# Four memory-attention heads turned so that queries lie on the partitions, in a one-core hybrid decoder step

## The chip, the cores and the metric

The kernel runs on one core of a Trainium2 chip. The metric is the device time of one execution in microseconds (us). The engines are called as in the profile: PE (TensorE matmuls), PEld (its weight loads), DVE (VectorE), ACT (ScalarE), POOL (GpSimd) and SP (SyncE, which issues most of the transfers).

## The reference, cut to what matters

One layer: a combined input projection, a gated convolution, eight dilated window-attention heads, four memory heads, a gate, one output projection, a residual and a final norm. The change touches the memory heads and the output projection's weights:

```python
def _mem_attn(qm, mk, mv):                       # 4 heads of 64, 2048 queries, 256 memory tokens
    s = jnp.einsum('bthe,bmhe->bhtm', qm, mk) * (HEAD_DIM ** -0.5)
    p = jax.nn.softmax(s, axis=-1)
    return jnp.einsum('bhtm,bmhe->bthe', p, mv)

def _finish(x, conv_y, attn_o, mem_o, z, w_out):
    mix = jnp.concatenate([conv_y, attn_o, mem_o], axis=-1) * jax.nn.silu(z)
    return x + mix @ w_out
```

## The kernel before, in words

After the projections come twelve "units": `Head` 0 to 7 (window attention) and `MemHead` 0 to 3. A unit has two parts, `scores()` and `values()`; while one unit's scores run, the values of the unit before it run too (`period`). A value is split into a high and a low half wherever a product has to be exact, so scores are two accumulating matmuls (`qk`), and an output product is three.

A memory head before the change keeps the 256 memory tokens on the partitions (two blocks of 128) and the queries along the row. Its maximum per query therefore runs across partitions. `Maxima.add` takes a transposing reduction on DVE (L765), `Maxima.finish` reduces again (L770), turns on PE (L772), reduces (L774), writes 4 KB to DRAM (`dmax`, L775) and reads it back to all partitions as `Rm` (L776). POOL then subtracts `Rm` (L1078), ACT takes the exponential (L1079), PE multiplies by the memory values (L1083), and `Sums` adds the weights over the partitions with matmuls against ones (L789). `finish_head` turns these sums, takes reciprocals, spreads and turns them again (L802 to L818), scales the output and stores it to `dmix` (L821).

The window heads use the same path for their maximum. Their POOL subtractions are L955, L956, L961, L976 and L977, their value products L950, their exponentials L957, L958, L962, L978, L982. `values()` of a head is cut by `yield` into places: the subtractions for the first half of `Rm` stand at place 0, `mx.finish(1)` and all other subtractions at 0.1, the products from 0.60 on.

Order: inside `tc.manual_schedule` (the periods of heads 1 to 7) PE and SP run in the order of the program text. On the other engines, and everywhere outside it, a planner fixes a static order per engine: among the instructions that are ready in its own model of time, the one that comes first in the text goes first. [...]

The tiles of even units come from `vals[0]` and `keys[0]`, those of odd ones from `vals[1]` and `keys[1]`. After the last unit the output stage starts: `load_wo` brings `w_out` in 16 pieces of 256 KB (L1188), splits each on ACT (L1189) and on DVE or POOL (L1190). `Rows` loads a block of mixed rows (`mx`, L1223), gates and splits it (L1224 to L1228), and runs 48 products a block over eight chunks (L1236, L1246); 17 blocks make 816 products. Row blocks 16, 0 and 1 start beside the last memory head:

```python
    interleave(units[-2].values(), lw, 6, 16)
    p2v.close()
    ow = ctx.enter_context(tc.tile_pool(name="ow", bufs=2, side="right", reuse_waits="tile"))
    ...
    interleave(units[-1].values(), first_rows(), 6, 80)
```

Of the kernel before, what the change touches and what calls it, by code (L numbers as in the profile page):

```python
# [18 lines left out]
D = 1024  # L19
T = 2048  # L20
# [6 lines left out]
EPS = 1e-6  # L27
SLOPE = [2.0 ** -(h + 1) for h in range(H)]
# [246 lines left out]
def tile_step(ctx, tc, x_prompt, x_sample, mem_prompt, ck, cv, cconv, cmk, cmv, g_in, w_in, conv_w,  # L275
# [448 lines left out]
    p2q = ctx.enter_context(ExitStack())  # L724
    vals[0] = p2v.enter_context(tc.tile_pool(name="vals0", bufs=1, side="right", reuse_waits="tile"))
# [15 lines left out]
    def q_load(row, turn):  # L741
        qh = keys[turn].tile([128, T], R, name="qh")
        ql = keys[turn].tile([128, T], R, name="ql")
# [286 lines left out]

    class MemHead:
        def __init__(self, h, turn):
            self.h, self.turn = h, turn

        def load_qk(self):
            h = self.h
            self.q = q_load(512 + h * 64, self.turn)
            self.mk = mk = keys[self.turn].tile([128, T], R, name="ks").rearrange("p (a b) -> p a b", b=128)[:, 0:2]
# [3 lines left out]
        def load_v(self):  # L1042
            pass
# [4 lines left out]
        def scores(self):  # L1048
            vp, mk, (qh, ql) = vals[self.turn], self.mk, self.q
            Rm = vp.tile([128, T], F, name="Rm")  # L1050
            mx = Maxima(self.turn, Rm, 2)
            S = {}
            for hf in range(2):
                for kb in range(2):
                    S[kb, hf] = vp.tile([128, 8, 128], F, name="S", bufs=4)
                for q in range(2):
                    for kb in range(2):
                        ps = psQ.tile([128, 4, 128], F, name="qk")
                        c = 1024 * hf + 512 * q
                        qk(ps, mk[:, kb], qh[:, c:c + 512], ql[:, c:c + 512])  # L1060
                        nc.scalar.activation(S[kb, hf][:, 4 * q:4 * q + 4], ps, AF.Copy)  # L1061
                    yield
                for kb in range(2):
                    mx.add(mx.parts[:, 32 * hf:32 * hf + 32, kb], S[kb, hf].rearrange("p r (x c) -> p (r x) c", c=32))
            self.S, self.Rm = S, Rm.rearrange("p (r b) -> p r b", b=128)
            for hf in range(2):
                mx.finish(hf)
                yield

        def values(self):  # L1070
            h, S, Rm = self.h, self.S, self.Rm
            po = psA.tile([128, 2, 512], F, name="acc")
            sums = Sums()
            o_sb = wk.tile([128, 8, 128], F, name="osb", bufs=1)
            o_v = o_sb.rearrange("p (a r) (J b) -> p r a J b", r=2, b=8)
            for hf in range(2):
                for kb in range(2):
                    nc.gpsimd.tensor_sub(S[kb, hf], S[kb, hf], Rm[:, 8 * hf:8 * hf + 8])  # L1078
                    nc.scalar.activation(S[kb, hf], S[kb, hf], AF.Exp)  # L1079
                yield 0.25 + 0.4 * hf  # L1080
                for kb in range(2):
                    for g in range(2):
                        nc.tensor.matmul(po[g * 64:(g + 1) * 64, hf], memv[:, kb, h * 64:(h + 1) * 64],  # L1083
                                         S[kb, hf][:, 4 * g:4 * g + 4].rearrange("p x y -> p (x y)"),
                                         start=(kb == 0), stop=(kb == 1), skip_group_check=True)
                nc.scalar.activation(o_v[:, hf], po[:, hf].rearrange("p (J a b) -> p a J b", a=4, b=8), AF.Copy)
            for kb in range(2):
                for r4 in range(4):
                    sums.add(r4, 0, 512, S[kb, r4 // 2][:, 4 * (r4 % 2):4 * (r4 % 2) + 4].rearrange("p x y -> p (x y)"), last=kb == 1)
            yield from finish_head(o_sb, sums, 768 + h * 64, 1.2)  # L1090
# [44 lines left out]
    units = [Head(h, h % 2) for h in range(H)] + [MemHead(h, h % 2) for h in range(HM)]  # L1135
# [6 lines left out]
    keys[1].pool = p2q.enter_context(tc.tile_pool(name="keys1", bufs=1, reuse_waits="tile"))  # L1142
    units[1].regroup(16, range(4))

    def loads(n):
# [3 lines left out]
        for k in range(2):  # L1149
# [3 lines left out]
            if k == 0:  # L1153
                units[n].load_v()
        for k in range(2):
# [10 lines left out]
    periods(H, len(units) - 1, 6)  # L1166
    advance(9.0)
    with tc.high_priority(350):
        for _ in units[-1].scores():
            pass  # L1170
# [4 lines left out]
    CH = range(8)  # L1175
    woh, wol = {}, {}

    room = [hT["A"][0].rearrange("p s c n -> p (s c n)")[:, D * i:D * i + D] for i in range(6)]
    for d in reversed(CH):
# [153 lines left out]
```

## Time and profile before

| what | us |
|---|---|
| median of 3 runs (lowest, highest) | 1350.94 (1350.39, 1357.62) |
| the profiled execution, its own time | 1356.83 |
| span of the profiled execution | 1354.8 |
| PE busy over the span | 1235.3 (91%) |
| stretch of the memory heads (1047 to 1172): PE busy of 125 us | 102.38 |

The profile counts an engine as busy while an instruction of its runs; a busy PE is not a PE at its peak, because matmuls overlap. "Idle before" is the time that an engine stood still in front of an instruction, with what released it. The granted clock (PEclk) is a share of 2.4 GHz, 0.50 being 1.2 GHz. Times within the trace count from the start of the span.

### The profile page before, as it was taken

The page shows a single profiled execution, that of the slowest core. Times are in us where ns is not written, and L with a number is a line of the kernel's source. Part 1 is how long each engine was busy: PE and PEld are TensorE (multiplying, and loading weights), DVE is VectorE, ACT ScalarE, POOL GpSimd, SP SyncE. Part 2 cuts the span into 40 slices and gives each one's busy share as a digit, 9 for nine tenths or more (in the row PEclk, how much of TensorE's full clock was granted, in tenths as well). Part 3 has the DMA queues.
Part 4 walks back from the last instruction along what each step waited for, and adds up shares of the span by engine and source line. Part 5 has one row for each costly group of instructions (what it writes and reads, how often), then busy time and mean ns, then how long its engine had stood idle before and what let it go on. Part 6 is the DMA issues. An engine that isn't in the chain of part 4 may idle for free. (4 is left out here: it accounts for less than half of the span.)

```text
span 1354.8 us, 20180 instructions
## 1 busy us (share of the span) xinstructions
PE 1235.3 (91%) x7814; PEld 991.2 (73%) x7814; DVE 643.6 (48%) x1201; ACT 435.8 (32%) x692; POOL 460.1 (34%) x398
## 2 busy tenths in 40 slices
PE   6999999999797779999999999898899877999997
PEld 5778898988696666777898787666666432778886
DVE  4544221156556750400451077777787235554442
ACT  4433132322232001011112217566665555421111
POOL 2130010155455510100470006666666656110000
PEclk9999999999898889999999999899999987999999
DMA  6453142378887437476555477888888856776641
GB/s 232 129 152 105 51 135 100 125 228 247 245 249 248 149 87 167 137 176 194 152 168 158 106 170 172 189 186 188 187 187 179 193 136 180 228 237 191 197 153 66
DMA packets 228103, 229.57 MB, mean 169 GB/s; under 512 B 67348, under 2 KB 182280, under 8 KB 223912
## 3 DMA queue, kind: packets, MB, share of 16 engines
q1 hardware_dynamic: 222248, 217.79, 58.9%
q10 hardware_dynamic: 5760, 10.49, 2.2%
q8 instruction: 62, 1.02, 0.3%
q14 instruction: 33, 0.27, 0.1%
HBM read 171.92 MB, written 56.31 MB: 168 GB/s over the span
## 5 line engine op out<-in xcount | busy, mean ns | idle before, releaser
L359 PE MATMUL b<-hA,whi 128*128 128x384 f32 (+1 forms) x1152 | 288.1, 328 | 7.7 <-DVE big L644 6.1
L359 PEld LDWEIGHTS b<-hA,whi 128*128 128x128 f32 x1152 | 204.7, 190 | 17.7 <-issue 7.0
L359 PE MATMUL b<-hA,wlo 128*128 128x384 f32 (+1 forms) x576 | 188.3, 327 | 0.0
L351 POOL TENSOR_TENSOR wlo<-wraw,whi 128x512 fp32r<-128x512 f32 x56 | 80.8, 1459 | 283.8 <-ACT whi L350 253.1
L359 PE MATMUL b<-hB_hi,whi 128*128 128x512 f32 (+1 forms) x416 | 165.2, 397 | 12.8 <-DVE big L688 8.4
L124 POOL TENSOR_TENSOR spr<-sk,sqb 128x512 f32<-128x512 f32 (+2 forms) x110 | 122.7, 1126 | 145.6 <-DMA sqb<-dqs 56.6
L359 PE MATMUL b<-hB_hi,wlo 128*128 128x512 f32 (+1 forms) x416 | 163.6, 393 | 0.0
L359 PE MATMUL b<-hB_lo,whi 128*128 128x512 f32 (+1 forms) x416 | 163.5, 393 | 0.0
L125 DVE TENSOR_REDUCE sc<-spr 128x8 f32<-128x512 f32 (+1 forms) x160 | 87.7, 571 | 66.5 <-POOL spr L124 66.2
L359 PEld LDWEIGHTS b<-hA,wlo 128*128 128x128 f32 x576 | 109.9, 191 | 4.4 <-issue 3.7
L828 DVE SCALAR_TENSOR_TENSOR S<-dt,b 128x128 f32<-128x128 f32 (+2 forms) x224 | 70.1, 355 | 90.1 <-PE b L825 51.1
L417 POOL TENSOR_TENSOR ss<-ss,nhalf 128x1 f32<-128x1 f32 (+1 forms) x34 | 20.8, 613 | 249.6 <-DVE ss L416 240.6
L359 PEld LDWEIGHTS b<-hB_hi,whi 128*128 128x128 f32 x416 | 80.0, 192 | 31.6 <-DVE big L688 9.2
L359 PEld LDWEIGHTS b<-hB_lo,whi 128*128 128x128 f32 x416 | 79.8, 192 | 19.3 <-issue 2.5
L359 PEld LDWEIGHTS b<-hB_hi,wlo 128*128 128x128 f32 x416 | 80.0, 192 | 17.7 <-issue 2.1
L961 POOL TENSOR_TENSOR S<-S,Rm 128x512 f32<-128x512 f32 x32 | 40.6, 1294 | 141.2 <-DVE S L828 61.4
L765 DVE TRANSPOSE_TENSOR_REDUCE mparts<-S 128x12 f32<-128x384 f32 (+1 forms) x96 | 76.3, 823 | 25.1 <-ACT S L1061 25.0
L695 ACT ACTIVATE ehi<-b 128x384 f32<-128x384 f32 (+2 forms) x40 | 20.7, 518 | 155.9 <-PE b L359 139.1
L1236 PE MATMUL b<-hA,mh 128*128 128x512 f32 x192 | 64.5, 392 | 3.7 <-DVE xo L1266 3.1
L557 DVE TENSOR_TENSOR elo<-big,ehi 128x512 fp32r<-128x512 f32 x24 | 22.4, 969 | 94.5 <-ACT ehi L556 78.6
L350 ACT ACTIVATE whi<-wraw 128x512 fp32r<-128x512 f32 x56 | 33.5, 625 | 92.9 <-PE b L359 87.9
L1236 PE MATMUL b<-woh,ml 128*128 128x512 f32 x160 | 62.8, 394 | 0.0
(250 smaller groups left out, 2412.9 us busy)
## 6 DMA issues: line engine op xcount, KB each, us to landing
sk<-in_cache_win_k_dram SPq DMA_DIRECT2D x72, 256.0 KB, 3.9
vq<-in_cache_win_v_dram SPq DMA_DIRECT2D x36, 512.0 KB, 5.7
wraw<-in_w_in_dram SPq DMA_DIRECT2D x48, 256.0 KB, 4.3
sqb<-dqs SPq DMA_DIRECT2D x48, 256.0 KB, 4.4
Rm<-dmax SPq DMA_DIRECT2D x24, 512.0 KB, 4.6
v<-out_dram SPq DMA_DIRECT2D x16, 512.0 KB, 5.4
zg<-dz SPq DMA_DIRECT2D x16, 512.0 KB, 4.0
xo<-in_x_prompt_dram SPq DMA_DIRECT2D x16, 512.0 KB, 4.5
```

Source lines behind the costliest of these rows:

```text
L124: E.tensor_mul(pr[:n, :width], kt, qt)
L125: nc.vector.tensor_reduce(dst, pr[:n, :width].rearrange("p (h e) -> p h e", e=64), axis=AX.X, op=OP.add)
L350: nc.scalar.activation(hi[:, a:a + 4], raw, AF.Copy)
L351: lo_eng.tensor_sub(lo[:, a:a + 4], raw, f32(hi[:, a:a + 4]))
L359: nc.tensor.matmul(ps, a(d), b(d), start=(n == 0), stop=(n == 23))
L417: nc.gpsimd.tensor_tensor(ss[:n], ss[:n], nhalf[:n], op=OP.pow)
L557: nc.vector.tensor_sub(lo, part, f32(hi))
L695: nc.scalar.activation(zt[:, :n], ps, AF.Silu)
L765: nc.vector.tensor_reduce(out, scores, axis=AX.X, op=OP.max, apply_transpose=True)
L828: nc.vector.scalar_tensor_tensor(S, dt, sl, ps, op0=OP.mult, op1=OP.add)
L961: nc.gpsimd.tensor_sub(S3[:, r4], S3[:, r4], mr[:, r4])
L1236: nc.tensor.matmul(self.ps[k], l[:, d], r[d][:, sl], start=first and i == 0, stop=last and i == 2)
```

## The change

A memory head now keeps 128 queries on the partitions and the 256 tokens along the row. It runs in four groups G of 512 queries. `weights(G)` does the scores with the queries as the stationary operand, takes the maximum along the row from PSUM on DVE, negates it, and lets ACT take the exponential with that bias and its sum (`accum_out`). The weights are scaled by the reciprocal sum, on POOL for even G (one product over 128x1024) and on DVE for odd G (four). `turn(G)` transposes the weights on PE, eight blocks a group, with one copy out of PSUM on ACT and one on DVE. `values(hf)` multiplies by the memory values for two groups and stores the result without any further scaling.

The four heads are one written-out loop of 19 steps inside the manual order of PE and SP, in which step n does `weights` of group n, `turn` of group n-2 and, at even n, `values` of the groups before that. The values of window heads 6 and 7 that are left are spread over these steps (`advance(0.09 * n)`). All four memory heads take their tiles from `vals[0]` and `keys[0]`. Output chunks 0 to 2 are loaded in steps 5 to 10; the other five are loaded after the loop, through two buffers instead of four, and the first row blocks come after all memory heads in the text.

```diff
+EARLY = (0, 1, 2)
...
+    psM, psMQ = Ring((4, 5)), Ring((2, 3))
+
     class MemHead:
...
         def load_qk(self):
-            h = self.h
-            self.q = q_load(512 + h * 64, self.turn)
...
+            h, k = self.h, self.h % 2
+            self.q = q_load(512 + h * 64, 0, *(("ks", "kr") if k else ("qh", "ql")))
...
-        def scores(self):
...
-        def values(self):
...
+        def weights(self, G):
...
+            P = self.P[G] = vals[0].tile([128, 4, 8, 32], F, name="S", bufs=4).rearrange("p t a b -> p t (a b)")
+            m, l = wk.tile([128, 4], F, name="mm"), wk.tile([128, 4], F, name="ml")
+            for i in range(2):
+                ps = psMQ.tile([128, 2, 256], F, name="qk")
+                for k in range(2):
+                    c = 512 * G + 256 * i + 128 * k
+                    nc.tensor.matmul(ps[:, k], qh[:, c:c + 128], mk, start=True, stop=False)
+                    nc.tensor.matmul(ps[:, k], ql[:, c:c + 128], mk, start=False, stop=True)
+                nc.vector.tensor_reduce(m[:, 2 * i:2 * i + 2], ps, axis=AX.X, op=OP.max)
+                nc.vector.tensor_scalar(m[:, 2 * i:2 * i + 2], m[:, 2 * i:2 * i + 2], -1.0, None, op0=OP.mult)
+                for k in range(2):
+                    t = 2 * i + k
+                    nc.scalar.activation(P[:, t], ps[:, k], AF.Exp, bias=m[:, t:t + 1], accum_out=l[:, t:t + 1])
+            nc.vector.reciprocal(l, l)
+            if G % 2:
+                for t in range(4):
+                    nc.vector.tensor_scalar(P[:, t], P[:, t], l[:, t:t + 1], None, op0=OP.mult)
+            else:
+                nc.gpsimd.tensor_mul(P, P, l.unsqueeze(2).to_broadcast([128, 4, 256]))
+
+        def turn(self, G):
...
             for kb in range(2):
...
+                pt = psM.tile([128, 4, 128], F, name="pt")
+                for t in range(4):
+                    nc.tensor.transpose(pt[:, t], self.P[G][:, t, 128 * kb:128 * kb + 128], ident)
+                out = self.PT[G // 2][:, 2 * (G % 2) + kb].rearrange("p (a b) -> p a b", b=128)
+                if kb:
+                    nc.vector.tensor_copy(out, pt)
+                else:
+                    nc.scalar.activation(out, pt, AF.Copy)
+
+        def values(self, hf):
...
+            po = psM.tile([128, 512], F, name="pt")
+            for kb in range(2):
+                for g in range(2):
+                    nc.tensor.matmul(po[g * 64:(g + 1) * 64], memv[:, kb, h * 64:(h + 1) * 64], self.PT[hf][:, 2 * g + kb],
+                                     start=(kb == 0), stop=(kb == 1), skip_group_check=True)
...
+        if n == H - 1:
+            yield 0.6
+            units[H + 1].load_qk()
+            return
...
-    periods(H, len(units) - 1, 6)
...
+        def load_wo(pool, chunks):
...
+                    raw = pool.tile([128, 512], F, name="woraw", bufs=2)
...
+        wo1 = ctx.enter_context(tc.tile_pool(name="wo1", bufs=1, reuse_waits="tile"))
+        lw = load_wo(wo1, EARLY)
+        streams.append([0.0, units[H - 1].values(), 0.0])
+        mem = units[H:]
+        for n in range(4 * HM + 3):
+            advance(0.09 * n)
+            if n < 4 * HM:
+                mem[n // 4].weights(n % 4)
+            if n in (4, 8):
+                mem[n // 4 + 1].load_qk()
+            if n >= 5:
+                next(lw, None)
+            if 2 <= n < 4 * HM + 2:
+                mem[(n - 2) // 4].turn((n - 2) % 4)
+            if n >= 4 and n % 2 == 0:
+                mem[(n - 4) // 4].values((n - 4) // 2 % 2)
+        advance(9.0)
...
+    with tc.high_priority(100):
+        for _ in lw:
             pass
...
+        for _ in load_wo(wo, [d for d in CH if d not in EARLY]):
+            pass
     p2v.close()
...
-    interleave(units[-1].values(), first_rows(), 6, 80)
+    for _ in first_rows():
+        pass
```

## Rows read from the trace of the kernel before

**Rows 1.** Chain that ended last, in order of time: start, us, what

```profile
1215.50 121.10 PE b L1236 x528
1336.61 11.00 PE b L1246 x48
```

**Rows 2.** Busy time by stretch: PE, PEld, DVE, ACT, POOL, then clock, DMA, GB/s

```profile
1047.00:1172.00 125.00, 102.38 (x653) 52.77 (x652) 53.72 (x76) 69.98 (x105) 67.84 (x40) 0.90 0.69 184
1098.00:1104.00 6.00, 1.14 (x4) 0.59 (x4) 1.25 (x1) 0.26 (x1) 1.83 (x1) 1.00 0.87 258
1104.00:1110.00 6.00, 3.86 (x12) 2.30 (x14) 1.51 (x3) 4.75 (x7) 6.00 (x4) 0.50 0.02 5
...
1172.00:1348.00 176.00, 172.48 (x752) 140.62 (x750) 79.19 (x99) 34.22 (x51) 10.84 (x16) 1.00 0.56 174
```

**Rows 3.** Timeline of SP: heads 6 and 7 store their maxima

```profile
1013.92 0.34 SPq L775 DMA_DIRECT2D dmax<-mc  x1
...
1047.67 0.53 SPq L775 DMA_DIRECT2D dmax<-mc  x1
```

**Rows 4.** Timeline of POOL: heads 6 and 7, then memory heads 0 and 3

```profile
1019.49 2.53 POOL L961 TENSOR_TENSOR S<-S,Rm 128x512 f32<-128x512 f32 x2 [10.07 <-DMA Rm<-dmax]
...
1060.81 2.48 POOL L961 TENSOR_TENSOR S<-S,Rm 128x512 f32<-128x512 f32 x2 [17.82 <-DMA Rm<-dmax]
...
1084.06 9.40 POOL L1078 TENSOR_TENSOR S<-S,Rm 128x1024 f32<-128x1024 f32 x4
...
1145.92 5.31 POOL L1078 TENSOR_TENSOR S<-S,Rm 128x1024 f32<-128x1024 f32 x2
```

**Rows 5.** Timeline of DVE and ACT: head 7's `Rm` late; later, row block 16

```profile
1060.65 0.21 DVE L810 RECIPROCAL rl<-b 128x16 f32<-128x16 f32 x1
...
1063.33 1.06 ACT L962 ACTIVATE S<-S 128x1024 f32<-128x1024 f32 x1 [4.66 <-POOL S L961]
1064.29 1.04 ACT L811 ACTIVATE rx<-rl 128x1024 f32<-128x1024 f32 x1
...
1147.03 1.97 DVE L1224 TENSOR_TENSOR mx<-mx,zg 128x256 f32<-128x256 f32 x1
```

**Rows 6.** Timeline of PE: 256-column pairs, four transposes, eight value products

```profile
1020.00 0.29 PE L824 MATMUL b<-hA,kr 128*128 128x256 f32 x1
1020.12 0.29 PE L825 MATMUL b<-hA,kr 128*128 128x256 f32 x1
...
1020.98 0.60 PE L807 MATMUL b<-ident,rx 128*128 128x128 f32 x4
1021.34 0.36 PE L824 MATMUL b<-hA,kr 128*128 128x256 f32 x1
...
1090.56 1.94 PE L1083 MATMUL acc<-S,memv 128*64 128x512 f32 x8
```

**Rows 7.** Busy time of PE, 1047 to 1098: first L950 alone, then L789

```profile
1047.00:1098.00 51.00, 15.67 (x256) 11.40 (x256) 0.97 0.79 182
...
1047.00:1098.00 51.00, 12.58 (x72) 2.12 (x72) 0.97 0.79 182
```

**Rows 8.** ACT and DVE: busy us and mean ns, or ns min/median/max

```profile
L1061 ACT ACTIVATE S<-b 128x512 f32<-128x512 f32 x32 | 18.0, 599 | 13.5 <-PE b L825 8.4 <-PE b L789 4.6 <-PE acc L1083 0.2
L958 ACT ACTIVATE S<-S 128x128 f32<-128x128 f32 x4 | 1.2, 306 | 1.0 <-POOL S L955 1.0
...
L1251 ACT ACTIVATION_READ_ACCUMULATOR sq<-xo x2: 185/186/186, 1343.5 to 1349.0; 128x1 f32 x2
...
L125 DVE TENSOR_REDUCE sc<-spr x160: 401/670/689, 275.4 to 711.2; 128x8 f32<-128x512 f32 x96, 128x4 f32<-128x256 f32 x64
```

**Rows 9.** Landing of `mx` after its issue (L1223), then gating and split

```profile
DMA to landing us min/median/max: 1.8/4.7/7.7
...
L1224 DVE TENSOR_TENSOR mx<-mx,zg 128x896 f32<-128x896 f32 x2 | 2.2, 1094 | 2.4 <-DMA mx<-dmix 2.4
L1227 ACT ACTIVATE mh<-mx 128x1024 fp32r<-128x1024 f32 x1 | 1.1, 1057 | 3.7 <-DVE mx L1224 3.7
```

More of the change, by code (lines that the diff above doesn't have):

```diff
@@ L739, in tile_step, with q_load @@
     d1 = dt1.rearrange("p (r J c) -> p r J c", r=4, J=2)
-    def q_load(row, turn):
-        qh = keys[turn].tile([128, T], R, name="qh")
-        ql = keys[turn].tile([128, T], R, name="ql")
+    def q_load(row, turn, hi="qh", lo="ql"):
+        qh = keys[turn].tile([128, T], R, name=hi)
+        ql = keys[turn].tile([128, T], R, name=lo)
         for g in range(2):
@@ L1039, in load_qk @@
             nc.sync.dma_start(f32(mk[0:64]).rearrange("p a b -> p (a b)"), dmk_hi[h * 64:(h + 1) * 64])
             nc.sync.dma_start(f32(mk[64:128]).rearrange("p a b -> p (a b)"), dmk_lo[h * 64:(h + 1) * 64])
-        def load_v(self):
-            pass
+            self.P, self.PT = {}, {}
         def regroup(self, d, parts):
             pass
-        def scores(self):
[L1049 to L1068, printed above, removed]
@@ L1070, in values @@
-        def values(self):
[L1071 to L1086, printed above, removed]
-            for kb in range(2):
-                for r4 in range(4):
-                    sums.add(r4, 0, 512, S[kb, r4 // 2][:, 4 * (r4 % 2):4 * (r4 % 2) + 4].rearrange("p x y -> p (x y)"), last=kb == 1)
-            yield from finish_head(o_sb, sums, 768 + h * 64, 1.2)
@@ L1133, in period @@
             x[2] += 1.0
-    units = [Head(h, h % 2) for h in range(H)] + [MemHead(h, h % 2) for h in range(HM)]
+    units = [Head(h, h % 2) for h in range(H)] + [MemHead(h) for h in range(HM)]
     units[0].load_qk()
@@ L1165, in tile_step @@
         periods(1, H, 24)
-    periods(H, len(units) - 1, 6)
[L1167 to L1170, printed above, removed]
+        p2k.close()
+        CH = range(8)
+        woh, wol = {}, {}
+        room = [hT["A"][0].rearrange("p s c n -> p (s c n)")[:, D * i:D * i + D] for i in range(6)]
+        def load_wo(pool, chunks):
+            for d in chunks:
+                for x in (woh, wol):
+                    x[d] = room.pop() if room else pool.tile([128, D], R, name="wo%d" % (2 * d + (x is wol)))
+            for d in chunks:
+                for k in range(2):
+                    raw = pool.tile([128, 512], F, name="woraw", bufs=2)
+                    sl = slice(k * 512, (k + 1) * 512)
+                    nc.sync.dma_start(raw, w_out[0][d * 128:(d + 1) * 128, sl])
+                    nc.scalar.activation(woh[d][:, sl], raw, AF.Copy)
+                    (nc.gpsimd if (2 * d + k) % 4 < 1 else nc.vector).tensor_sub(wol[d][:, sl], raw, f32(woh[d][:, sl]))
+                    yield
@@ L1192, in tile_step @@
     with tc.high_priority(100):
-        lw = load_wo()
-        for _ in range(8):
-            next(lw)
-    interleave(units[-2].values(), lw, 6, 16)
+        for _ in lw:
+            pass
+        for _ in load_wo(wo, [d for d in CH if d not in EARLY]):
+            pass
     p2v.close()
```

45 lines of the change are left out of this document (26 added, 19 removed).

## The prediction

> **What bounds the kernel now.** I read the page first: PE is busy 91% of the span, so a saving has to take work off PE or close its gaps. The chain that ended last is almost only the output products: it reaches back 121.10 us over 528 of them, then 48 more up to 1347.6 [rows 1]. That gives a pitch of 121.10 / 528 = 0.2294 us, so all 816 products take 187.2 us without a gap and would start at 1347.6 - 187.2 = 1160.4. After 1172 PE stands still for 176 - 172.48 = 3.5 us, 0.4 of it after the last product [rows 2]; I keep the other 3.1. The output stage therefore behaves as if it started, dense, at **1157.3**. That is the number to move. Whatever moves it moves the end by as much, since the products after it are untouched.
>
> Next I read the stretch in front of it. From 1047, where head 7's scores end, to 1172 PE is busy 102.38 of 125 us, and the mean clock is 0.90 [rows 2]. The reader should see two things there. PE is idle for 22.6 us, and after one of the gaps (busy 1.14 of 6 us) the granted clock is 0.50, 1.2 GHz, in the next stretch [rows 2]. The timeline of POOL says what the gaps wait for: POOL stood still 17.82 us until head 7's `Rm` landed, then ran head 7's subtractions without a pause from 1060.81 to 1084.06, 23.25 us, and went straight on to memory head 0 [rows 4].
>
> **What goes, what comes.** I count from 1047 to the dense start.
>
> Removed for the memory heads: 32 copies out of PSUM at 0.60 us on ACT [rows 8], 16 subtractions at about 2.35 us on POOL [rows 4], the transposing reductions, eight trips of the maximum through DRAM, the sums on PE and the whole `finish_head`. None of it is priced alone, because the new stage is summed afresh.
>
> PE's new work. A group has eight score matmuls of 256 columns at a pitch of 0.12 us, 0.96 us; eight transposes at 0.36 us for four, 0.72 us; and every second group eight value instructions, 1.94 us [rows 6]. The first pitch is from pairs that load 128x128 weights before each matmul, as the new ones must. For 16 groups this is 26.9 us and eight times 1.94 is 15.5 us; with some 0.08 us for each change of kind (an estimate from 0.20 instead of 0.12 behind the transposes) 45.6 us. The window heads' rest stays: L950 15.67 us, L789 12.58 less 1.92 that belong to memory head 0 [rows 7], and 3.5 us of transposes: 29.8 us, of which about 2 are due to a lower clock, so 28. Together **73.6 us**. If nothing else counted, the products could start at 1121.
>
> ACT: 64 exponentials over 256 columns, which lie between 306 ns (128 columns) and 599 ns (512), about 0.40, and for each a reading of the accumulator of 0.186 [rows 8]. With a copy of 0.60 per group and half of one for the values this is 4 x 0.59 + 0.9 = 3.3 us a group, 52 us in all, and some 14 us for head 7. DVE: two reductions of 0.67 [rows 8] and a copy of like size per group, four scalings at 0.2 to 0.4 in odd groups, small ones: 2.6 to 4.0 us, about 53 us. Both are under PE's 73.6, so I cost them at nothing by themselves. That cover is thin: without the window heads' work a step of PE is 2.9 us and a step of ACT 3.3.
>
> POOL: eight products over 128x1024. The nearest row is 9.40 / 4 = 2.35 us [rows 4]; a broadcast operand could cost more, a smaller read less. I take 2.35.
>
> The wait that is added. PE now keeps the order of the text: `turn(n-2)` waits for the scaled weights of that group, and behind it stand the next scores and head 7's products. POOL has its own static order. Head 7's subtractions for the first half stand before step 0 in the text, and all others before `weights(2)`. Once these are ready they go first, so that POOL is busy with them from the landing of `Rm` for 23.25 us. That a static order costs time when `Rm` is late is seen on ACT: L811's input was there at 1060.86, but L962 stood in front of it and kept ACT until 1063.33 [rows 5]. So I expect PE to be held at an even group, 2 or 4, until head 7's subtractions and one product are done.
>
> When is that? Head 6's first maxima left at 1013.92 and its subtractions began at 1019.49, 5.6 us later; head 7's took 1047.67 to 1060.81, 13.1 us, with memory head 1's queries on the same queues [rows 3, 4]. Those are now issued earlier, at place 0.6 of head 7's period, and collide less. I take 9 us, keeping 5.6 and 13.1 as bounds: 1056.7 + 23.25 + 2.35 = 1082.3. Until then PE can do 14 us if it is held at group 2 and 19.5 if at group 4; I take 17. What remains is 73.6 - 17 = 56.6, up to 1138.9.
>
> Three additions. Seven value products come right behind a copy from the same pair of banks, 0.60 us and a hand-over [rows 8], 0.8 each: 5.6 us. After some 20 us of standing still PE starts at 0.50, as it did after 1098 [rows 2]: 3 us. So the last value product ends at about **1147.5**. Then the first row block has to be loaded. Its tiles lie where the memory heads' tiles were, and all four heads now use that pool: if they overlap the last head's weights, 4.7 us for `mx` [rows 9], 0.4 for gating, 0.7 for clearing, 1.06 for the split on ACT [rows 9], 6.9 in all; if they fall on tiles that no memory head uses, 0.3. I take 5. The dense start is then 1152.5.
>
> Of the gating, a row shows 1.97 us for 256 columns, beside 1.09 for 896, while POOL was in its subtractions [rows 4, 5, 9]. The Trainium skill ("SBUF — State Buffer", "Who interferes with whom") says that a DVE instruction with two SBUF inputs and a GpSimd instruction that reads SBUF take one shared port in turn, the later one blocked until the other is through. The trace agrees with it here. By that rule the 0.4 holds, because the subtractions are gone by then; by the 1.97 the sum would be 1.6 us longer. The same page lets a scaling on DVE into this contention, which speaks against putting the odd groups there; at one POOL product per two groups it would add at most 2.35 us to DVE's 6.6 for two groups, under PE's 10, so the sum is the same by either.
>
> The early weights: six pieces in steps 5 to 10, 3.8 us of ACT (the 0.60 row) and some 4 of DVE, under PE's slack. SP waits at the third piece for the first one's split, and memory head 3's queries stand behind it; they are wanted at step 12, so this costs nothing unless a step shrinks below about 2 us. The other ten pieces use two buffers. At one `mx`-like landing (4.7) and 1.3 of splitting per two, 3 us each, they take 30 us from about step 15, ten us before the end of the stage. Row blocks 16, 0 and 1 have 132 products, 30 us, that follow chunk by chunk, so this too is covered; with strict order of the blocks it would cost up to 8 us.
>
> Sum: 1157.3 - 1152.5 = 4.8 us less than the profiled execution (1356.83), 1352.0. That execution is 5.9 us above the median of the runs shown; against 1350.94 the forecast is **1346.1 us**.
>
> **Rivals.** *PE is not held* (faster). If POOL's order lets each group's product go as soon as it is ready, PE works on through the steps: 1047 + 73.6 + 5.6 plus some 7 us in which ACT or DVE, nearly as full, keeps a step waiting, 1133; plus 6.9, a dense start at 1140, 17 us earlier: 1334. For it: POOL is idle until `Rm` lands, so group 0's product may well be in front. Against it: group 2's comes after 23.25 us of older work.
>
> *PE is held at group 0* (slower). If POOL's order has head 7's first subtraction in front of group 0's product, PE stops at the first `turn`, with 10.6 us done. With `Rm` as late as before, 1060.8 + 23.25 + 2.35 = 1086.4, then 63 us and 8.6: 1158, and 6.9: 1164.9, which is 7.6 us later: 1358.5. It decides from the point where that subtraction stands first in POOL's order. For it: the reductions that feed group 0 queue on DVE behind head 7's last maxima.
>
> *Nothing gained*: held at group 2 with `Rm` late, all bounds at their long ends, 1350 to 1354. That is the upper end of my own case.
>
> **How the numbers follow.** Held at group 2 or 4: 0.50, its own range 1338 to 1354. Not held: 0.25, 1328 to 1341. Held at group 0: 0.18, 1350 to 1364. Others, such as a stall on the late weights: 0.07, mostly slower. 0.5% of 1350.94 is 6.8 us, about what a measurement of this kernel can tell from no change. Below 1344.2 lie all of the second case and 0.38 of the first: 0.44. Above 1357.7 lie two thirds of the third and most of the rest: 0.19. Within: 0.37. The range that holds eight in ten reaches to both other cases: 1330 to 1360.
>
> **What would show it.** Right: a gap of PE of 10 us or more in front of a transpose of memory head 0 or 1, released by POOL's product; POOL unbroken over head 7's subtractions for 23 us; a clock of 0.50 behind the gap; PE idle for some us between the last value product and the first output product. Wrong: no gap of PE over 5 us before 1120 (not held), a gap already at the first transpose (group 0), the output products waiting for weights (L1189), or ACT busy without a break through the loop, which would make its 3.3 us a step the bound.

## The result, and the profile after

The changed kernel took 1389.7 us (median of 4 runs, 1387.36 to 1391.77) against 1352.06 us for the kernel before on the same chip: a ratio of 1.027, 95% interval 1.0235 to 1.0305. It is slower by 2.7%, where 1346.1 us and a small gain had been forecast; 1389.7 lies 30 us above the upper end of the range.

The first view is the busy time by stretch in the kernel after (PE, PEld, DVE, ACT, POOL, then clock, DMA, GB/s). I cut it at the first memory score on PE (1043.80), at the end of the first POOL hold (1082.26), at the end of the last value product (1167.89), and at the first and last output product.

```profile
1043.80:1082.26 38.46, 16.01 (x113) 12.10 (x110) 22.40 (x37) 16.95 (x48) 27.22 (x22) 0.67 0.52 120
1082.26:1167.89 85.63, 65.77 (x516) 43.24 (x516) 41.30 (x108) 46.87 (x136) 14.19 (x9) 0.85 0.36 82
1167.89:1183.60 15.71, 0.04 (x1) 0.04 (x1) 4.61 (x7) 4.58 (x7) 2.22 (x2) 0.66 0.98 247
1183.60:1378.39 194.79, 194.08 (x816) 154.37 (x816) 85.07 (x104) 35.87 (x54) 9.75 (x16) 0.98 0.54 169
```

From the first memory score to the last output product it is 1378.39 - 1043.80 = 334.6 us. Before, the like stretch ran from 1047.4, its first memory score, to 1347.6 [rows 1], 300.2 us. The stretch is thus 34.4 us longer, and the loss lies in the loop and at its end. (The medians differ by 37.6, the spans of the two profiled runs by 30.7: where the stretch starts varies from run to run, 1043.8 here and 1049.4 in e1, which is the same up to there.) PE is busy for about as long as before, 275.9 us over these four rows against 102.38 + 172.48 = 274.9 [rows 2], in part at a lower clock; almost the whole loss is time in which PE stands still. In the loop of 124.1 us PE is busy for 81.8 and idle for 42.3. The groups of that stretch, for PE, say what ended the idle time (busy us and mean ns, then idle us and the releasers):

```profile
L1083 PE MATMUL b<-ident,S 128*128 128x128 f32 x128 | 20.9, 318 | 8.3 <-POOL S L1073 8.0 <-ACT S L1088 0.3
L1061 PE MATMUL b<-mk,qh 128*128 128x256 f32 x32 | 11.2, 368 | 20.3 <-ACT S L1067 20.3
L1061 PE MATMUL b<-mk,ks 128*128 128x256 f32 x32 | 10.5, 351 | 4.7 <-ACT S L1067 4.7
L1101 PE MATMUL b<-S,memv 128*64 128x512 f32 x32 | 10.3, 773 | 7.0 <-ACT Rm L1088 7.0
L1101 PE MATMUL b<-Rm,memv 128*64 128x512 f32 x32 | 8.6, 664 | 1.9 <-ACT S L1088 1.6 <-ACT Rm L1088 0.3
```

So 25.0 us are scores that wait for an exponential on ACT to free their PSUM buffer (where PE writes its products), 8.0 are transposes that wait for POOL's scaling, 8.9 are value products behind a copy on ACT. The timeline shows what ACT itself was waiting for. Each line has start, us, engine, and in brackets the idle time before it with its releaser.

```profile
1043.18 0.34 SPq L777 DMA_DIRECT2D dmax<-mc  x1
1051.11 0.36 SPq L778 DMA_DIRECT2D Rm<-dmax  x1
...
1054.98 2.48 POOL L963 TENSOR_TENSOR S<-S,Rm 128x512 f32<-128x512 f32 x2 [16.35 <-DMA Rm<-dmax]
...
1061.81 1.89 POOL L1073 TENSOR_TENSOR S<-S,ml 128x1024 f32<-128x1024 f32 x1
...
1080.27 1.94 POOL L1073 TENSOR_TENSOR S<-S,ml 128x1024 f32<-128x1024 f32 x1
...
1049.88 0.19 ACT L1067 ACTIVATION_READ_ACCUMULATOR S<-b,mm 128x1 f32 x1
1057.50 1.06 ACT L964 ACTIVATE S<-S 128x1024 f32<-128x1024 f32 x1 [7.42 <-POOL S L963]
1058.46 0.46 ACT L1067 ACTIVATE S<-b,mm 128x256 f32<-128x256 f32 x1
...
1067.78 0.47 ACT L1067 ACTIVATE S<-b,mm 128x256 f32<-128x256 f32 x1 [5.07 <-DVE S L1071]
...
1112.30 0.63 ACT L1204 ACTIVATE hA<-woraw 128x512 fp32r<-128x512 f32 x1 [4.43 <-DMA woraw<-in_w_out_dram]
...
1061.78 5.88 DVE L1071 TENSOR_SCALAR S<-S,ml 128x256 f32<-128x256 f32 x4
...
1098.86 1.15 DVE L1071 TENSOR_SCALAR S<-S,ml 128x256 f32<-128x256 f32 x4
...
1059.06 0.58 PE L1061 MATMUL b<-mk,qh 128*128 128x256 f32 x1 [7.79 <-ACT S L1067]
1063.75 1.97 PE L1083 MATMUL b<-ident,S 128*128 128x128 f32 x8 [2.55 <-POOL S L1073]
...
1082.26 1.97 PE L1083 MATMUL b<-ident,S 128*128 128x128 f32 x8 [5.42 <-POOL S L1073]
1089.22 3.68 PE L1101 MATMUL b<-S,memv 128*64 128x512 f32 x8 [4.99 <-ACT Rm L1088]
...
1113.89 0.58 PE L1061 MATMUL b<-mk,qh 128*128 128x256 f32 x1 [4.24 <-ACT S L1067]
...
1183.57 1.22 PE L1272 MATMUL b<-hA,mh 128*128 128x512 f32 x2 [15.72 <-ACT mh L1263]
```

Three things are to be read off. First, the static order that held POOL is on ACT too. Head 7's first exponential (L964) stands between two exponentials of one memory group, waits 7.42 us for a POOL subtraction that waits for `Rm`, and PE is held for 7.79 us by the exponential behind it. POOL then serves one scaling at 1061.81 and the next only at 1080.27, after all of head 7's subtractions. Second, four scalings on DVE take 5.88 us while POOL works and 1.15 when it is idle, and ACT stands for 5.07 us behind them. Third, a split of an early output weight (L1204) stands in ACT's order before its load has landed, 4.43 us, and holds PE for 4.24. The six loads landed 9.4 us (median) after their issue, some of them issued right behind 2 MB of memory queries.

At the end of the loop, the chain of waits has the first row block's mixed rows, and after it only output products, as in [rows 1]:

```profile
1176.30 5.61 DMA mx<-dmix
1184.83 35.06 PE b L1272 x139
1221.79 145.40 PE b L1272 x622
1367.18 11.22 PE b L1282 x48
```

The last value product ended at 1167.89, `mx` was issued 8.4 us later and landed 5.61 us after that; gating, clearing and the split made up the rest of 15.7.

### The profile page after: what moved, and what is told of

Same layout as the page of the kernel before. It is cut to its first block, busy times and chain, and to the rows that moved or that the text cites. A ratio compares the mean times of both kernels' runs of the same rounds, so it can differ in the third digit from the quotient of the medians.

```text
span 1385.5 us, 20475 instructions
## 1 busy us (share of the span) xinstructions
PE 1242.3 (90%) x7886; PEld 1012.9 (73%) x7886; DVE 665.9 (48%) x1285; ACT 436.5 (32%) x780; POOL 433.9 (31%) x390
## 4 chain that ended last, share of the span: by engine, by line
PE 61%; DMA 20%; DVE 7%; ACT 5%; POOL 3%; issue 3%; SPq 1%; DVEq 0%; POOLq 0%; ACTq 0%
PE b L360 30%; PE b L1272 13%; DMA sk<-in_cache_win_k_dram 7%; PE acc L952 5%; PE b L826 3%; DMA vq<-in_cache_win_v_dram 3%; PE b L827 2%; DMA sqb<-dqs 2%; PE b L791 2%; DMA xt<-in_x_prompt_dram 2%; DMA woraw<-in_w_out_dram 2%; PE acc L167 2%; DVE spr L125 2%; POOL spr L125 1%; DMA Rm<-dmax 1%
## 5 line engine op out<-in xcount | busy, mean ns | idle before, releaser
L1272 PE MATMUL b<-wo,mh 128*128 128x512 f32 x320 | 106.3, 396 | 0.0
L1272 PE MATMUL b<-hA,mh 128*128 128x512 f32 x192 | 66.8, 404 | 15.7 <-ACT mh L1263 15.7
L1272 PEld LDWEIGHTS b<-wo,mh 128*128 128x128 f32 x320 | 60.3, 189 | 14.9
L1272 PE MATMUL b<-wo,ml 128*128 128x512 f32 x160 | 63.3, 396 | 0.0
```

Of the source, the lines that this page charges most:

```text
L1272: nc.tensor.matmul(self.ps[k], l[:, d], r[d][:, sl], start=first and i == 0, stop=last and i == 2)
```

## The experiments

Times are ratios to the kernel before, run on the same chip. "Stretch" runs from the first memory score to the last output product of the profiled run (e6 and e8, where head 7 is finished before that score: from head 7's first `dmax` store). "Loop" ends with the last value product, "gap" with the first output product. Stretch, loop and gap come from one profiled run of each kernel. Only the ratios of e13, e14 and e16 lie well clear of after's interval; the kernels from e1 to e12 are told apart mainly by their stretches, whose spread from run to run was not measured.

| kernel | ratio (95%) | stretch | loop | gap |
|---|---|---|---|---|
| before | 1 | 300.2 | | |
| after | 1.027 (1.0235 to 1.0305) | 334.6 | 124.1 | 15.7 |
| e1_no_early | 1.0229 (1.0187 to 1.0271) | 324.0 | 111.4 | 16.7 |
| e2_scale_act | 1.0312 (1.027 to 1.0353) | 339.4 | 130.6 | 15.1 |
| e3_q_early | 1.0295 (1.0249 to 1.0341) | 334.6 | 123.8 | 16.0 |
| e4b_last_vals1 | 1.0239 (1.0198 to 1.028) | 326.1 | 124.1 | 3.5 |
| e10_head0_act | 1.0188 (1.0142 to 1.0234) | 328.6 | 117.6 | 16.6 |
| e7_both | 1.0195 (1.0149 to 1.024) | 328.4 | 112.4 | 5.3 |
| e6_serial | 1.0303 (1.0257 to 1.0348) | 345.1 | 89.5 | 17.4 |
| e8_serial_both | 1.0197 (1.0139 to 1.0255) | 331.9 | 73.7 | 5.6 |
| e11_text | 1.0311 (1.0288 to 1.0334) | 338.1 | 140.9 | 0 |
| e12_all | 1.0238 (1.0221 to 1.0255) | 331.9 | 138.9 | below 0 |
| e13_steps | 1.005 (1.0027 to 1.0074) | 303.3 | 104.7 | below 0 |
| e14_adv | 1.0011 (0.9997 to 1.0025) | 301.5 | 105.7 | below 0 |
| e16_both | 0.9954 (0.9937 to 0.9971) | 293.9 | 97.6 | 0.8 |

Where the gap is below 0, the first row block started before the last value product, and the loop holds some of its output products.

**No early weights (e1).** The 16 pieces of the output weights are all loaded after the loop.

```diff
-EARLY = (0, 1, 2)
+EARLY = ()
```

> No output weights are loaded inside the loop; all 16 pieces come after it. In the trace of the changed kernel ACT stood still 12.5 us in the loop in front of the early pieces' copies (4.43 + 3.10 + 2.70 + 2.30) with exponentials behind them, and PE lost 8.3 us in two gaps of 4.24 and 4.05 there. If the early copies on ACT are a cause, the last value product ends 8 to 10 us earlier than the 1167.85 of the changed kernel (1157 to 1160), and ACT shows no idle on a weight's landing before 1150. If PE is held only by POOL behind head 7's subtractions, it ends within 3 us of 1167.85. The total need not fall by either, since all pieces now come late through two buffers: 16 x 3 = 48 us of loading from about step 15 on, so 1378 to 1400.

Its loop, up to the end of the POOL hold (1088) and behind it:

```profile
1049.40:1088.00 38.60, 18.02 (x114) 13.42 (x113) 23.98 (x38) 17.28 (x49) 27.25 (x22) 0.65 0.48 113
1088.00:1160.79 72.79, 60.26 (x515) 39.19 (x513) 37.32 (x102) 42.51 (x129) 12.63 (x7) 0.93 0.34 76
```

Up to the end of the hold nothing changes (38.6 against 38.5). Behind it the same work of PE takes 72.8 instead of 85.6, and the clock is 0.93 instead of 0.85. The early weights thus cost 12.8 us of loop, though ACT's six splits are less than 4 us of work: 7.3 us are idle time of PE, and 5.5 are longer busy time for the same work at the lower clock. The ratios moved by 0.4% only, with intervals that overlap; the stretch of the one profiled run is the finer reading.

**Odd groups scaled on ACT (e2), and memory head 0 alone (e10).**

```diff
             if G % 2:
                 for t in range(4):
-                    nc.vector.tensor_scalar(P[:, t], P[:, t], l[:, t:t + 1], None, op0=OP.mult)
+                    nc.scalar.activation(P[:, t], P[:, t], AF.Copy, scale=l[:, t:t + 1])
```

That is e2. e10 has the same four copies on ACT for every group of head 0, odd and even, and leaves the other heads as they were.

> The odd groups' scaling goes from DVE to ACT (four copies with a scale). In the changed kernel DVE's four scalings took 5.88 and 5.58 us in groups 1 and 3, while POOL subtracted, and 1.14 us in later groups; ACT then stood still 5.07 and 5.25 us in front of the exponentials. If DVE and POOL take turns at a port, these two waits go: 5 to 10 us off the stage, last value product at 1158 to 1163, total 1379 to 1385. If the hold is POOL's order alone, the four scalings on ACT (0.4 us each, 13 us in all) add to ACT and the end moves by less than 3 us: 1387 to 1393.

> Only memory head 0's four groups are scaled on ACT, so that in the time of head 7's subtractions POOL has no product that PE waits for and DVE no scaling that shares a port with POOL; heads 1 to 3 stay as they are. In the changed kernel PE stood still 2.55 and 5.42 us for POOL's products, and DVE's scalings of 5.88 and 5.58 us delayed ACT and PE by some 9 us more. If PE is held by POOL as forecast, the loop falls from 124.1 to 106 to 114 us and the total to 1371 to 1381. If it is ACT's order behind head 7's late maxima (7.79 us in front of group 1's second half) and what follows, the loop stays above 118 and the total above 1383.

e2 is no faster and so nearer its second case, but its loop is 6.5 us longer than after's: ACT's work in the loop rises from 63.8 to 76.2 us, and PE waits 9.71 us for POOL's product of group 2, where it waited 5.42. e10 takes POOL and DVE out of the first four groups only, and the loop is 6.5 us shorter, 117.6, between the two cases of its expectation; PE's 8.0 us of waiting for POOL's product are gone, and its wait behind L964's place in ACT's order is 10.2 us instead of 7.8. So the two scalings beside POOL and POOL's own product are together worth some 6 us, and the hold by ACT's order stays.

**Memory head 1's queries earlier (e3).** They are issued at place 0.2 of head 7's period instead of 0.6.

```diff
         yield 0.2
         units[n + 1].load_qk()
+        if n == H - 1:
+            units[H + 1].load_qk()
```

> Memory head 1's queries (2 MB) are loaded at place 0.2 of head 7's period, together with head 0's, and not at 0.6, just in front of head 7's first maxima. In the changed kernel the 4 KB of those maxima took 7.87 us to land behind them, and ACT stood still 7.42 us in front of head 7's first exponential, PE 7.79 us. If the late maximum is a cause, the 4 KB land in about 2 us, POOL starts its subtractions near 1049 and not at 1055, and the total falls by 5 to 6 us, to 1383 to 1385. If PE is bound further down by POOL's 23 us and the rest, some 2 us of it remain: 1386 to 1389. If the window head's values come later because of the 2 MB in front of them, it is slower: over 1391.

The timeline of SP:

```profile
1033.70 12.61 SPq L853 DMA_DIRECT2D v<-out_dram  x4
...
1050.09 0.59 SPq L777 DMA_DIRECT2D dmax<-mc  x1
1052.84 0.35 SPq L778 DMA_DIRECT2D Rm<-dmax  x1
```

`Rm` now follows its store by 2.75 us instead of 7.9, but the store itself stands behind the loads of head 7's values and leaves 5.1 us after the first memory score instead of 0.6 before it. POOL's first subtraction begins 11.7 us after that score (11.2 in after). The wait moved along SP's queue, much as the last case of the expectation had it, and the stretch is the same: when `Rm` lands is set by the whole queue, not by these loads.

**The last memory head's tiles from vals[1] (e4b), and both (e7).**

```diff
-                self.PT[1] = vals[0].tile([128, T], F, name="Rm").rearrange("p (g b) -> p g b", g=4)
+                self.PT[1] = vals[self.h // 3].tile([128, T], F, name="Rm").rearrange("p (g b) -> p g b", g=4)
```

The head's other four tiles are moved in the same way. e7 is e4b with e1's edit.

> The last memory head takes its weights, turned weights and output tile from head 7's pool, so that the pool over which the output rows' tiles lie is free one head earlier. In the changed kernel PE stood still 15.72 us between the last value product and the first output product, whose mixed rows were asked for only at 1176.30. If this gap is the tiles' release, the rows are asked for before the last value product ends, the gap falls to 0 to 4 us, and the total falls by 10 to 16 us: 1374 to 1380. If it is SP's queue (row loads behind weight pieces that wait for one of two buffers), the gap stays above 8 us and the total falls by less than 6: 1384 to 1390.

> No early weights, and the last memory head in head 7's pool: two changes that each shortened the stretch from the first memory score to the last output product, by 10.6 and by 8.5 us. If they act on different waits (ACT behind early weights inside the loop; row tiles behind it), they add: 334.6 - 19 = 315 us for the stretch, 1370 to 1376 in all. If both only move the same late weights, the second gives nothing any more because all 16 pieces now have to come after the loop: 322 to 326, 1379 to 1387.

With e4b the first row block no longer waits for tiles of the last memory head. The gap falls from 15.7 to 3.5 us, the loop stays at 124.1, and the products give 3.7 back (198.5 against 194.8). The time fell less than expected, to 1388.3 us, and the ratios of the two overlap. In e7 the two gains do not add: the stretch is 6.2 us under after's, not 19.1. The output products of e7 take 210.7 us, 12.3 of which PE stands still: 6.6 for weights that are not there yet, with all 16 pieces late, and 5.7 for mixed rows not yet split. Three of the waits for weights, from its timeline:

```profile
1194.15 0.50 PE L1272 MATMUL b<-wo,mh 128*128 128x512 f32 x1 [0.18 <-ACT wo L1204]
1196.83 0.50 PE L1272 MATMUL b<-wo,mh 128*128 128x512 f32 x1 [1.02 <-ACT wo L1204]
1201.34 0.80 PE L1272 MATMUL b<-wo,mh 128*128 128x512 f32 x1 [2.84 <-ACT wo L1204]
```

So the early weights are of use to the products; whether they hurt by their place in ACT's order is what e12 tries.

**Head 7 finished first (e6, and e8 with e7's edits).** The memory heads run alone behind head 7.

```diff
         mem = units[H:]
+        advance(9.0)
         for n in range(4 * HM + 3):
```

> Everything that is left of the window heads is put in front of the 19 memory steps instead of being spread over them; nothing else is changed. It measures the new memory heads by themselves. In the changed kernel the stretch from the first memory score to the last output product took 334.6 us (300.2 in the kernel before), its loop 124.1. If the loop is long because PE, ACT and DVE queue behind head 7's late weights, the 19 steps now run at their own pace, some 3.0 us of PE and 3.3 of ACT each, 55 to 62 us, and window rest plus steps take about 45 + 58 = 103: the loop is over some 20 us earlier and the total is 1365 to 1375. If the new steps are long by themselves (scores, maximum, exponential, transposes in a row, 5 us or more a step), the steps take 85 us or more and the total is 1390 or more.

> The two changes of the run before, and the window heads' rest in front of the steps. If interleaving behind head 7's late weights is the main loss, this is the best of the new form: stretch 290 to 302, total 1352 to 1362. If the late weights and rows bound it, no better than the run before: stretch 312 or more, 1370 or more.

Busy time over the 19 steps alone, e6 and then e8:

```profile
1093.20:1182.69 89.49, 59.99 (x323) 39.66 (x321) 54.13 (x136) 48.95 (x160) 17.83 (x10) 0.85 0.45 103
```

```profile
1090.50:1164.19 73.69, 53.17 (x323) 36.00 (x320) 50.07 (x132) 45.48 (x153) 16.41 (x9) 0.95 0.51 109
```

Alone, a step takes 73.69 / 19 = 3.9 us in e8, with PE busy for 2.8; in e6, with the early weights, it is 4.7, and its 89.5 us fall under the case "long by themselves". The memory heads' own PE work is 53 us, not the 45.6 that I had worked out. Finishing head 7 first costs as much as it saves: e8's loop is 38.7 us shorter than e7's, and head 7's values, which now stand before it alone, push its start back by 42.8 us; the ratios are the same.

**The order of the text on all engines (e11, e12).** Head 7's subtractions and exponentials come from step 3 on, two parts a step, the scalings behind the turn, and the last head's tiles come from `vals[1]` as in e4b; e12 also splits each early weight one step after its load was issued.

```diff
     with tc.manual_schedule(engines={PE, SP}):
         periods(1, H, 24)
+    with tc.manual_schedule(engines={PE, SP, Activation, Pool, DVE}):
         ...
             if 2 <= n < 4 * HM + 2:
                 mem[(n - 2) // 4].turn((n - 2) % 4)
+            if n < 4 * HM:
+                mem[n // 4].scale(n % 4)
```

> Edit: in the loop of the memory heads all five engines keep the order of the text; head 7's subtractions and exponentials are written out from step 3 on, two parts a step, each exponential one step behind its subtraction; the scalings of a group stand behind the turn of that step; the last memory head takes its tiles from vals[1], as in e4b. Measured from head 7's first dmax store to the last output product, before took 299.9 us, after 335.2 and e4b 326.8. Theory (the loss of the loop is a static order that puts head 7's late work ahead of the first groups): the gaps of 7.8, 2.6 and 5.4 us at the start go, no ACT idle of 7 us before head 7's first exponential, loop 124 -> 95 to 105 us, stretch about 300 to 308, time 1352 to 1362. Rival (the loop is long because each step's chain score, maximum, exponential, copy takes 3.9 us by itself, as in e8, and head 7's work adds to it): loop 112 to 120, stretch above 315, time above 1368. Rival 2 (DVE's scalings beside POOL's subtractions bound it): a scaling of 5 to 6 us in three odd steps with PE idle behind each, loop 108 to 115.

> Edit: e11, and each early piece of the output weights is split one step after its load was issued (two buffers as before). Theory (ACT stands in front of a split whose load has not landed, with the exponentials of the step behind it): the idle times of ACT before L1204's split, 2.3 to 4.4 us in after, go, and the loop is 5 to 10 us shorter than e11's; the output products are as in e4b, so the time is below e11's by as much, 1345 to 1355. Rival (what the early weights cost is the splitting itself on ACT and DVE, or their traffic beside the query loads): loop within 3 us of e11's.

e11 was a miss of mine: its loop is longer than after's. The old gaps went and new ones came, at nearly every pair of value products, as PE's timeline of e12 shows:

```profile
1092.25 3.54 PE L1136 MATMUL b<-Rm,memv 128*64 128x512 f32 x8 [4.20 <-ACT S L1123]
...
1107.37 3.68 PE L1136 MATMUL b<-S,memv 128*64 128x512 f32 x8 [4.46 <-ACT Rm L1123]
1110.84 4.46 PE L952 MATMUL acc<-S,v 128*64 128x256 f32 x48
```

The value product needs the PSUM bank of the turn in the same step, and in the text that turn's copy stands on ACT behind the four exponentials of the step. Then a lump of head 7's products, 9 us, kept PE from the next scores. That both kernels read the text in order was not enough; the text had to be in a good order. e12's loop is 2.0 us shorter than e11's, within the 3 us that the rival gave it, but the two loops do not hold the same work: in e12 the first row block begins 8.5 us before the last value product, and PE is busy for 5.6 us more (94.8 against 89.2) with its first products. Up to the first output product it is 130.4 us in e12 and 140.9 in e11, and the stretch is 6.2 us shorter. ACT's waits for the early loads, 1.6, 3.3 and 4.5 us in e11, are gone in e12. The delayed split thus did what it was meant to; how much of the 6.2 us is its own, and how much the earlier row block's, is not separated. The time fell by 0.7%, and the intervals do not overlap.

**The step turned round (e13), head 7 behind the scores (e14), room for the late weights (e16).** e13's step is: one part of head 7, value products of the last pair, turn three groups behind, scores of this step, scaling of the group before; POOL scales the first 13 groups.

```diff
+        for n in range(4 * HM + 4):
+            advance(0.09 * n + 0.001)
...
+            g = n - 4
+            if g >= 1 and g % 2:
+                mem[g // 4].values(g % 4 // 2)
+            g = n - 3
+            if 0 <= g < 4 * HM:
+                mem[g // 4].turn(g % 4)
             if n < 4 * HM:
                 mem[n // 4].weights(n % 4)
+            if 1 <= n <= 4 * HM:
+                mem[(n - 1) // 4].scale((n - 1) % 4)
```

In e14 the line with `advance` stands between `weights` and `scale`. e16 is e14 with other tiles for the late weights (the early ones keep their two buffers):

```diff
-                    raw = pool.tile([128, 512], F, name="woraw", bufs=2)
+            raw2 = vals[0].tile([128, 4, 8, 32], F, name="S", bufs=4).rearrange("p t a b -> p (t a b)")
```

> Edit: as e12 (text order on all five engines, early weights split one step after their load, last head's tiles from vals[1]), with the text of a step turned round: first one part of head 7's subtractions, the exponential of the part before it and one part of head 7's products, then the value products of the pair finished in the step before, then the turn (now three groups behind), then the scores, maxima and exponentials, then the scaling of the group before. The first 13 groups are all scaled on POOL. Theory (e11 and e12 were slow because the value products stood behind an ACT copy of the same step, 4 to 8 us a pair, and head 7's products lay in one lump of 9 us): these two gaps go, PE is idle for less than 20 us from head 7's first dmax store on, loop 90 to 105 us, stretch (before 299.9, e12 332.5) 290 to 305, time 1347 to 1362. Rival (each step is a ring score, maximum, exponential, copy, with two PSUM buffers each, that takes 4 us or more whatever is laid beside it, and head 7's work lengthens it): loop above 115, stretch above 312, time above 1370.

> Edit: as e13, with head 7's part of a step (subtractions, an exponential, products) put behind the scores, maxima and exponentials of the step instead of in front of it. Theory (in e13 each pair's second turn waits 1.1 to 2.6 us for the value copy on ACT, which stands behind head 7's exponential, and that one for POOL): these five gaps, 8.8 us together, shrink to under 1 us each; loop about 95 to 100 us, stretch 5 to 9 us under e13's 303.9, time about 1354 to 1359. Rival (PE waits as long at the next scores, since the step's ring is ACT's and DVE's): the gaps move to the scores, stretch within 3 us of e13's.

> Edit: as e14, and the ten late pieces of the output weights are loaded into the four score tiles of vals[0], which no memory head uses any more by then (two pieces a tile, so eight pieces can be under way instead of two). Theory (two buffers make the late weights trickle in at 3 us a piece, and the first output products wait for them): PE's waits for L1265's splits behind 1130, in e13 6.1, 2.8 and 0.9 us, go, and the clock stays at 1.00 there; stretch 8 to 12 us under e14's, time below before by up to 0.5 to 1%. Rival (the output stage is limited by the bytes of w_out beside zg, mx and xo, or by the mixed rows of head 7, stored late): stretch within 3 us of e14's.

The loop of e13, and then the loop and the products of e16:

```profile
1050.00:1154.69 104.69, 83.58 (x658) 57.50 (x655) 56.22 (x125) 64.73 (x188) 54.81 (x37) 0.90 0.61 147
```

```profile
1040.10:1137.69 97.59, 76.84 (x620) 51.17 (x618) 61.09 (x127) 66.71 (x191) 56.86 (x38) 0.91 0.62 153
...
1138.50:1333.99 195.49, 193.00 (x819) 154.05 (x816) 83.62 (x103) 34.94 (x52) 9.71 (x16) 0.99 0.54 170
```

With the memory heads' computation unchanged, the order on ACT, POOL and DVE, the place of the scalings, the split one step later and the tiles of the last head take the ratio from 1.027 to 1.005 (e13). From e12 to e13, which differ in the order of a step, in how finely head 7's work is cut and in where the scalings are done, it falls by 1.9%, 25 us; no kernel tells these three apart. e14 did not do what it was meant to: the waits for the value copy stayed, 10.6 us instead of 8.8, and the stretch is 1.8 us shorter, as its rival had it. Its ratio is 0.4% lower, some 5 us, and the rest of that is not explained. e16, in which only the tiles of the late weights differ, shows what those cost: 7.6 us of stretch less than e14, no wait of PE for a split of the weights any more (3.8 us in e14), and the time falls below the kernel before, by 0.5% (interval 0.3 to 0.6). (Of the waits that its expectation counts, the one of 6.1 us ends on a turn's copy, which on ACT stood behind a split that had waited 2.68 us for its load.) What is left is again a place in ACT's order, the copy of the values (e13, e14 and e16 in turn):

```profile
L1140 PE MATMUL b<-ident,S 128*128 128x128 f32 x128 | 20.1, 295 | 13.3 <-ACT v L1161 8.8 <-POOL S L1130 4.4
...
L1140 PE MATMUL b<-ident,S 128*128 128x128 f32 x128 | 21.4, 306 | 15.4 <-ACT v L1161 10.6 <-POOL S L1130 4.4 <-DVE Rm L1143 0.2
...
L1140 PE MATMUL b<-ident,S 128*128 128x128 f32 x128 | 20.0, 292 | 14.8 <-ACT v L1161 11.0 <-POOL S L1130 3.5 <-DVE Rm L1143 0.3
```

## Why the prediction was wrong, by its own steps

The forecast's stretch was 100.5 us to the last value product (1047 to 1147.5), 5 of row start, and 190.3 of products (1347.6 - 1157.3), 295.8 in all. Measured were 124.1, 15.7 and 194.8. The differences are 23.6, 10.7 and 4.5, together 38.8.

**The anchor held, with one correction.** The products stayed one dense block behind a start that moves. They took 4.5 us more and 3.2 of these are the first 27: they ran at a mean granted clock of 0.66, after 15.7 us in which PE stood still, and took 9.4 us, where 27 x 0.2294 is 6.2.

**The hold was right in size and end, and only in part in its cause.** I had PE held at even group 2 or 4 with some 17 us done, up to 35.3 us after the start. Measured: 16.0 us done when the hold ended, at the transposes of group 2, 38.5 us after the start. POOL ran without a break, as forecast: six of head 7's subtractions, group 0's product, the other subtractions, group 2's product. But PE was stopped several times on the way, by ACT and DVE too; POOL alone accounts for 8.0 us, and the longest gap that it ended was 5.42 us, not the 10 or more that was named as the sign. That the size came out is thus partly luck. Of `Rm`, 9 us was taken and 11.8 came, inside the bounds; that is most of the 3.2 us.

**"Both are under PE's 73.6, so I cost them at nothing by themselves" is the step that failed.** Behind the hold I had 56.6 of work, 3 for the clock and 5.6 for copies, 65.2; it took 85.6, 20.4 more. The sums of busy time were near enough for ACT (63.8 against some 66) and 11 us low for DVE (63.7 against 53), both well under the loop of 124; but nothing in such sums says that ACT is free when the next exponential is ready. The early weights, "3.8 us of ACT, under PE's slack", cost 12.8 of the 20.4 (e1): the splits stand in front of exponentials and wait 12.5 us for their loads, which queue on SP behind memory queries with two buffers, and behind the gaps the clock is lower. How much of this comes from the wait at SP that I noted, and priced at nothing, was not measured. The other 7.6 are what e1 has left there, 72.8 against 65.2: 60.3 of work where 59.6 had been summed with the clock, and 12.5 of idle time where 5.6 had been kept for copies. The sum of PE's work was near (78.3 in e1's loop against 73.6 and 3), though its parts were not: the memory heads alone take 53 us (e8), not 45.6.

**I had the mechanism and used it for one engine.** The text cites L811 behind L962 as proof that a static order costs time on ACT when `Rm` is late, and then applies it to POOL alone. L964 between two exponentials of one group is the same thing. (The row shows more than the text says: L962 only began at 1063.33, and L811 had ACT at 1064.29.)

**The odd scalings.** They were priced at 0.2 to 0.4 us each and "at most 2.35 us" of contention per two groups. Four of them took 5.88 and 5.58 us beside POOL's subtractions, and 1.15 alone, so the size was right without POOL (0.29 each) and the bound was wrong with it. The Trainium skill ("SBUF — State Buffer", "Who interferes with whom") lets a scaling on DVE enter the contention for the port that it shares with GpSimd; the trace agrees, with 5.88 against 1.15. The error was to charge one wait for one POOL product, although POOL read SBUF without a pause during all four. Moved to ACT by themselves they saved nothing (e2); together with POOL's product it was 6.5 us of loop (e10).

**The row start: 5 us, measured 15.7.** That its tiles overlap the last head's is right (e4b: 3.5 us without the overlap). The 6.9 for this case left out that `mx` is issued only 8.4 us after the last value product; in its queue late weights and other loads of the row stand in front of it.

**The rivals.** "Held at group 0" had its condition right, since head 7's first subtractions stood in front of group 0's product, and the sign of the change. At that first `turn` PE waited only 2.55 us, because ACT's order had already stopped it for 7.79 at the scores in front. It gave 1358.5 against 1389.7, for the same reason: what lies behind the hold. Late weights cost nothing here (PE is busy for 194.08 of 194.79 us), as forecast, but only since the products start so late: in e7, with an earlier start and all pieces late, PE waits 6.6 us for them, and in e14 3.8.

What stays open: e14 shows that the value copy still stops PE, and no kernel gave it another engine or bank; how much faster than e16 the new form can be is not known.

## What to carry to other kernels

Work that fits under another engine's busy time is hidden only if the order of that engine lets it wait: for each instruction added to an engine with a static order, name what its input waits for and what stands behind it, and charge that wait to whoever needs the next one. Where a change puts a short ring (score, maximum, exponential, copy) on engines that also serve late work of the stage before, write out their order together and look at each place where a copy stands behind work of a later step; between e12 and e13, where the scalings moved too, 25 us were gained. A gap costs twice: behind the one of 15.7 us the clock was 0.66 and 27 products took 9.4 us instead of 6.2.

## What the runs showed of the hardware

Four scalings of 128x256 on DVE took 5.88 us beside POOL's subtractions against 1.15 alone, and in e8, where those subtractions are over before the steps, no group's four took more than 1.15. POOL's 128x512 subtractions took 1.25 to 1.31 us beside the scalings and 1.25 to 1.28 away from them: nearly the whole cost fell on DVE. And the price of the clock could be read from two loops with 323 matmuls each on PE: 59.99 us busy at a mean granted clock of 0.85 (e6), 53.17 at 0.95 (e8).
